# Attention values as one run of 256-column pairs, two buffers of turned units, and the queries turned in the projection's bank

## The chip, the cores and the metric

One core of a Trainium2 chip runs the whole kernel. Its engines are TensorE (PE: matmuls and transposes, with its weight loads on PEld), VectorE (DVE), ScalarE (ACT), GpSimd (POOL) and SyncE (SP, which issues most transfers). Each works through its own list of instructions in order and waits at semaphores for the others. The metric is the device time of one execution in microseconds.

## The reference

One block of a hybrid network over 512 latent tokens and 256 context tokens, width 1024: a state-space scan and an attention beside it share one input projection and one output projection; then a mixture of experts. The change touches only the attention over 768 keys (context and latent) with 16 query heads in 4 groups, and what of the output projection follows it:

```python
def one_block(q_blk):
    s = jnp.einsum('bqhgd,bkhd->bhgqk', q_blk, k, preferred_element_type=F32) * scale
    pr = jax.nn.softmax(s, axis=-1).astype(v.dtype)
    return jnp.einsum('bhgqk,bkhd->bqhgd', pr, v)
```

## The kernel before, in words

The stages follow one another: input projection and scan, attention, experts. `attention()` (L896) works on 16 units, each a pair of a key group `kv` and a tile `t` of 128 queries (the table `order`); a unit has four heads. The loop at its end runs over steps of one head, and `step(i, start, n)` says which unit is at a stage that begins `start` steps after the unit's first head:

- step 0: `scores(u, g)`. Four matmuls write 768 columns of scores into one of two slots of `pss_`; the slots share the middle one of three PSUM banks. DVE takes the row maximum (L956), ACT the exponential with the row sum (L957), into `P`. At the second head `q_stack` prepares the next unit's queries (POOL L923, ACT L925, DVE L926); at the fourth `q_turn(u + 1)` transposes them (L934) in a bank "b", and ACT copies them out twice (L936, L937).
- step 2: `turn(j)`. P of four heads is 24 blocks of 128 x 128; six groups of four are transposed (L963) into a bank "b" and copied to `PT` by DVE (L967) or ACT (L965) in turn. A group can straddle two heads.
- steps 4 and 6: `values(u, j)`. For two heads at a time, 12 matmuls of 128 columns: the heads `2j` and `2j+1` go to the upper and lower 64 columns of the array.
- steps 6 and 7: `norms` (reciprocal sums) and `finish` (scaling by a transposed copy of them, L992 to L999).
- steps 9 and 10: `project(u, n)`, six matmuls of 512 columns into bank "t" (for the last two units into `pss_`), which DVE adds to the running sum (L1017).

`pb(tag)` hands out PSUM banks: there are two banks "b", and one each of "t" and "s". A bank is handed to its users in the order in which the program asks for it, and each waits until the one before has been read. Bank "t" has other users: the eight tiles of `out_group(1, n)` (L814, twelve matmuls each, added by DVE at L830), which is the scan's share of the output projection; and near the end the transposes, logits and tables of the expert router. The tiles of `out_group(1, n)` are written in the program ahead of the call of `attention()` (L1249):

```python
    at = tc.cur_priority
    for n in range(2):
        with rank(at + LAG):
            out_group(1, n)
```

The order on each engine is not the order of the program text: a scheduler takes the instructions by priority (`rank` sets it) and by when it expects them to be ready, and so strews the tiles of `out_group(1, n)` among the first units' heads. Which user of a bank comes first is fixed by the text all the same. `mm` (L109) is the helper through which most matmuls go, so its rows are told apart by their tiles: `s<-kT,hxl` or `s<-hxl` are scores, `v<-hxh,hxl` and `s<-hxh,hxl` values, `t<-whi,a` and `t<-wlo,a` out_group(1), `t<-whi,ah`, `t<-ml,ah` and the like projections.

## Time and profile before

| | |
|---|---|
| three runs | 889.95, 896.88, 919.74 us; median 896.88 |
| profiled execution | 891.73 us, span 889.9 us |
| mean granted TensorE clock | 0.967 |
| busy | PE 798.8 us (90%), DVE 630.3 (71%), ACT 455.0 (51%), POOL 268.0 (30%) |
| chain that ended last | PE 59%, DMA 14%, DVE 11%, ACT 6% |
| attention | first exponential at 409.57 us of the span, last at 647.52 |

The busy shares are means over stages with different limits: in the input projection and in the experts transfers of weights run at over 300 GB/s, in attention at far less. So the windows of attention are read by themselves, and its time is counted from exponential to exponential (L957), 64 of them, four a unit; the exponential of unit u's head g is number 4u + g from 0.

### The profile page before, as it was taken

What the parts mean: (1) busy time and instruction counts of PE and PEld (TensorE: products, weight loads), DVE (VectorE), ACT (ScalarE), POOL (GpSimd) and SP (SyncE); (2) the same over time, 40 slices, a digit from 0 to 9 for tenths busy, and PEclk for the clock granted to TensorE, in tenths of its full rate; (3) what the DMA queues carried; (4) which work ended last, traced back from release to release, by engine and by line L of the source; (5) the groups of instructions that cost most, each with busy time, mean ns of one, the idle gap of its engine ahead of it and who ended that gap; (6) DMA issues with size and microseconds to landing.
All of it is one profiled execution on the core that took longest, in us unless ns stands there. A gap on an engine that the chain in (4) does not pass through costs nothing.

```text
span 889.9 us, 14409 instructions
## 1 busy us (share of the span) xinstructions
PE 798.8 (90%) x5328; PEld 604.5 (68%) x5328; DVE 630.3 (71%) x1042; ACT 455.0 (51%) x870; POOL 268.0 (30%) x202
## 2 busy tenths in 40 slices
PE   6998999898989989899999899999982999999783
PEld 3696676566777568677777777787862777777562
DVE  3576665786857896573646566666987999889677
ACT  2253442656743353364544645656461766777452
POOL 0012212313321052510159344600011355544421
PEclk8999999999999999999999999999995999999997
DMA  9966987446522144566052111300459999999964
GB/s 308 321 193 230 299 292 251 124 125 199 144 73 80 30 130 131 194 197 207 18 194 73 36 35 42 119 13 1 143 195 324 343 342 341 338 325 344 341 181 167
DMA packets 112369, 165.59 MB, mean 186 GB/s; under 512 B 13032, under 2 KB 78088, under 8 KB 112296
## 3 DMA queue, kind: packets, MB, share of 16 engines
q1 hardware_dynamic: 105720, 141.76, 49.2%
q0 software_dynamic: 6288, 21.84, 8.6%
q8 instruction: 42, 0.69, 0.3%
q10 hardware_dynamic: 288, 1.05, 0.3%
q14 instruction: 31, 0.25, 0.1%
HBM read 142.41 MB, written 22.21 MB: 185 GB/s over the span
## 4 chain that ended last, share of the span: by engine, by line
PE 59%; DMA 14%; DVE 11%; ACT 6%; issue 5%; POOL 3%; SPq 1%; DVEq 0%; POOLq 0%; ACTq 0%
PE a L109 24%; PE s L109 13%; PE t L109 7%; PE b L963 3%; DMA wraw<-in_w_mod_dram 3%; PE v L109 3%; PE b L109 3%; DMA bc<-csd 2%; PE m L109 2%; DVE acc L475 2%; ACT hxh L957 1%; PE b L1368 1%; DMA wraw<-in_w_up_dram 1%; DMA ml<-in_w_down_dram 1%; DMA ml<-in_w_up_dram 1%
## 5 line engine op out<-in xcount | busy, mean ns | idle before, releaser
L76 ACT ACTIVATE whi<-wraw 128x1024 fp32r<-128x1024 f32 (+1 forms) x100 | 104.2, 1045 | 62.7 <-PE a L109 31.9
L78 DVE TENSOR_TENSOR wlo<-wraw,whi 128x1024 fp32r<-128x1024 f32 (+1 forms) x75 | 95.7, 1282 | 29.3 <-ACT whi L76 29.3
L78 POOL TENSOR_TENSOR wlo<-wraw,whi 128x1024 fp32r<-128x1024 f32 (+1 forms) x20 | 49.3, 2464 | 150.6 <-ACT whi L76 132.2
L956 DVE TENSOR_REDUCE mx<-s 128x1 f32<-128x768 f32 x64 | 61.1, 955 | 29.6 <-PE s L109 24.4
L957 ACT ACTIVATE hxh<-s,mx 128x768 f32<-128x768 f32 x64 | 57.5, 898 | 41.1 <-DVE mx L956 39.5
L475 DVE SCALAR_TENSOR_TENSOR acc<-u,cols,acc 128x770 f32<-128x770 f32 (+1 forms) x48 | 55.4, 1153 | 30.3 <-ACT acc L467 24.3
L109 PE MATMUL a<-whi,hxh 128*128 128x512 f32 (+2 forms) x176 | 69.1, 394 | 1.5 <-ACT hxh L265 1.5
L109 PE MATMUL a<-wlo,hxh 128*128 128x512 f32 (+2 forms) x176 | 69.1, 393 | 0.2 <-DVE wlo L78 0.2
L109 PE MATMUL a<-whi,hxl 128*128 128x512 f32 (+2 forms) x176 | 67.9, 387 | 0.0
L109 PE MATMUL a<-hxh,whi 128*128 128x512 f32 (+1 forms) x176 | 62.5, 355 | 0.0
L109 PE MATMUL a<-hxl,whi 128*128 128x512 f32 (+1 forms) x176 | 62.2, 354 | 0.0
L109 PE MATMUL a<-hxh,wlo 128*128 128x512 f32 (+1 forms) x176 | 61.7, 350 | 0.0
L963 PE MATMUL b<-cst,hxh 128*128 128x128 f32 x384 | 58.7, 277 | 1.7 <-DVE hxh L967 0.5
L592 ACT ACTIVATE bc<-bc,lb 128x128 f32<-128x128 f32 x128 | 40.5, 390 | 23.6 <-POOL bc L589 20.4
L963 PEld LDWEIGHTS b<-cst,hxh 128*128 128x128 f32 x384 | 43.5, 141 | 11.4 <-ACT hxl L937 4.0
L967 DVE COPY hxh<-b 128x512 f32<-128x512 f32 x48 | 33.0, 687 | 16.9 <-PE b L963 16.7
L109 PE MATMUL a<-whi,xh 128*128 128x512 f32 x102 | 44.4, 436 | 0.0
L589 POOL TENSOR_SCALAR_AFFINE_SELECT bc<-bc 128x512 f32<-128x512 f32 x32 | 26.5, 835 | 52.4 <-DMA bc<-csd 50.4
L109 PE MATMUL a<-whi,xl 128*128 128x512 f32 x102 | 41.3, 405 | 0.0
L109 PE MATMUL a<-wlo,xh 128*128 128x512 f32 x102 | 41.2, 404 | 0.0
L1417 POOL DMA_INDIRECT acc<-y,rowi x15 | 28.2, 1881 | 40.8 <-DVE wlo L78 19.4
L109 PEld LDWEIGHTS a<-wlo,hxh 128*128 128x128 f32 x176 | 33.8, 192 | 9.9 <-issue 5.3
(467 smaller groups left out, 2123.2 us busy)
## 6 DMA issues: line engine op xcount, KB each, us to landing
wraw<-in_w_mod_dram SPq DMA_DIRECT2D x32, 512.0 KB
wraw<-in_w_in_dram SPq DMA_DIRECT2D x30, 512.0 KB
wraw<-in_w_down_dram SPq DMA_DIRECT2D x22, 512.0 KB
wraw<-in_w_gate_dram SPq DMA_DIRECT2D x40, 256.0 KB
wraw<-in_w_up_dram SPq DMA_DIRECT2D x40, 256.0 KB
mraw<-in_w_mod_dram SPq DMA_DIRECT2D x32, 256.0 KB
bc<-csd SPq DMA_DIRECT2D x32, 256.0 KB
wraw<-in_w_out_dram SPq DMA_DIRECT2D x15, 512.0 KB
```

Source lines behind the costliest of these rows:

```text
L76: self.nc.scalar.activation(hi, raw, AF.Copy)
L78: self.lo_engine(i).tensor_sub(lo, raw, hi.bitcast(F32))
L109: return PE.matmul(o, lhsT=a, rhs=b, start=first, stop=last)
L475: V.scalar_tensor_tensor(a, uk, wk_, a, op0=OP.mult, op1=OP.add)
L589: G.affine_select(bc[:, d], bc[:, d], pattern=[[0, 4], [sg, 128]], compare_op=OP.is_ge, fill=-1e30, base=0, channel_multiplier=-sg)
L592: S.activation(bc[:, d, h, :], bc[:, d, h, :], AF.Exp, bias=lb[:, c, h0 + h:h0 + h + 1])
L956: V.tensor_reduce(m, x, axis=AX, op=OP.max, negate=True)
L957: S.activation(P[:, g * 768:g * 768 + 768], x, AF.Exp, bias=m, accum_out=sm[u][:, g:g + 1])
L963: PE.transpose(p[:, i * 128:(i + 1) * 128], P[:, (4 * j + i) * 128:(4 * j + i + 1) * 128], ident)
L967: V.tensor_copy(PT[:, o], p)
L1368: PE.transpose(p[:, j * 128:(j + 1) * 128], x[:, k * 128:(k + 1) * 128], ident)
L1417: G.indirect_dma_start(out=acc, out_offset=bass.IndirectOffsetOnAxis(ap=rows, axis=0), in_=y, in_offset=None, compute_op=OP.add)
```

## The change

- `turn(u, g)` works on one head, one step after it: two groups of three transposes, the first copied by DVE, the second by ACT (384 columns each).
- `P` becomes a ring of two heads in a tile of its own; the room that it had holds a second buffer of turned units.
- `values(u)` runs once all four heads are turned, at step 5: 12 matmuls of 256 columns (two heads beside each other), key blocks in reverse, into one column half of the array and the other in turn.
- `norms` and `finish` move to steps 5 and 6; heads 0, 1 now lie in one half and 2, 3 in the other, so the sums and the weight rows of the output projection are arranged to match (`attn_piece`: two transfers of 64 partitions each for a weight piece instead of one).
- `q_turn(u)` for u > 0 takes bank "t" instead of one of the banks "b".

```diff
 
+    def attn_piece(kv, n):
+        def views(t):
+            for gp in range(2):
+                r = 1024 + kv * 256 + gp * 128
+                yield t[gp * 64:gp * 64 + 64], I["w_out"][r:r + 128, n * 512:n * 512 + 512].rearrange(
+                    "(j d) n -> d j n", j=2)
+        return views, 2, 512
+
     def scaled(i, w):
...
     wout = Stream(nc, wp, [piece(4 * g + k0, n) for g in range(2) for n in range(2) for k0 in (0, 2)]
-                  + [piece(8 + 2 * kv, n) for kv in range(4) for n in range(2)], 1, 2, held=1, scale=scaled,
+                  + [attn_piece(kv, n) for kv in range(4) for n in range(2)], 1, 2, held=1, scale=scaled,
                   lo_engine=lambda i: V if i < 8 else G, place=place,
...
         big = hxp.tile([128, 6144], F32, name="hxh")
-        P, PT = (big[:, o:o + 3072] for o in (0, 3072))
-        PTh = PT.rearrange("p (g k q) -> p g k q", g=4, k=6)
+        PT = [big[:, o:o + 3072] for o in (0, 3072)]
+        PS = 2
+        Ps = wo.tile([128, 768 * PS], F32, name="P", bufs=1)
         more = hxp.tile([128, 6144], F32R, name="hxl")
...
         def q_turn(u, qs):
-            p = pb("b", F32R)
+            p = pb("t", F32R) if u else pb("b", F32R)
             for g in range(4):
...
             V.tensor_reduce(m, x, axis=AX, op=OP.max, negate=True)
-            S.activation(P[:, g * 768:g * 768 + 768], x, AF.Exp, bias=m, accum_out=sm[u][:, g:g + 1])
-
-        def turn(j):
-
-            p, o = pb(), slice(j * 512, (j + 1) * 512)
-            for i in range(4):
-                PE.transpose(p[:, i * 128:(i + 1) * 128], P[:, (4 * j + i) * 128:(4 * j + i + 1) * 128], ident)
-            if j % 2:
-                S.activation(PT[:, o], p, AF.Copy)
-            else:
-                V.tensor_copy(PT[:, o], p)
+            at = (4 * u + g) % PS * 768
+            S.activation(Ps[:, at:at + 768], x, AF.Exp, bias=m, accum_out=sm[u][:, g:g + 1])
+
+        def turn(u, g):
+
+            at = (4 * u + g) % PS * 768
+            for h in range(2):
+                p, o = pb()[:, 0:384], slice(g * 768 + h * 384, g * 768 + h * 384 + 384)
+                for i in range(3):
+                    f = at + (3 * h + i) * 128
+                    PE.transpose(p[:, i * 128:(i + 1) * 128], Ps[:, f:f + 128], ident)
+                if h:
+                    S.activation(PT[u % 2][:, o], p, AF.Copy)
+                else:
+                    V.tensor_copy(PT[u % 2][:, o], p)
 
...
 
-        def values(u, j):
+        def values(u):
 
             kv = order[u][0]
-            if j == 0:
-                po[u] = pb("s") if u % 2 else pss.tile([128, 512], F32, name="v")
-            for k in range(6):
-                for a in range(2):
-                    mm(po[u][a * 64:a * 64 + 64, j * 128:j * 128 + 128], vv[:, k, kv * 64:(kv + 1) * 64],
-                       PTh[:, 2 * j + a, k], k == 0, k == 5)
+            po[u] = pb("s") if u % 2 else pss.tile([128, 512], F32, name="v")
+            w = PT[u % 2].rearrange("p (g k q) -> p g k q", g=4, k=6)
+
+            for k in reversed(range(6)):
+                for a in (1, 0):
+                    mm(po[u][a * 64:a * 64 + 64, 0:256], vv[:, k, kv * 64:(kv + 1) * 64], w[:, 2 * a:2 * a + 2, k], k == 5, k == 0)
 
...
             V.reciprocal(rc, sm.pop(u))
-            rcb = wo.tile([128, 4, 64], F32, name="rcb", bufs=1)
-            S.activation(rcb, rc[:, :, None].to_broadcast([128, 4, 64]), AF.Copy)
-            return rcb.rearrange("p g d -> p (g d)")
+            rcb = wo.tile([128, 2, 2, 64], F32, name="rcb", bufs=1)
+            S.activation(rcb, rc.rearrange("p (g j) -> p j g", j=2)[:, :, :, None].to_broadcast([128, 2, 2, 64]), AF.Copy)
+            return rcb
 
...
             for j in range(2):
-                PE.transpose(p[:, j * 128:(j + 1) * 128], rcb[:, j * 128:(j + 1) * 128], ident)
+                PE.transpose(p[:, j * 128:(j + 1) * 128], rcb[:, j].rearrange("p g d -> p (g d)"), ident)
             rb = wo.tile([128, 256], F32, name="rb")
...
                     q_turn(u + 1, qs.pop(u + 1))
-            u, g = step(i, 2, 4)
+            u, g = step(i, 1, 4)
             if u is not None:
-                for j in ((0,), (1, 2), (3,), (4, 5))[g]:
-                    turn(j)
-            u, g = step(i, 4, 3)
-            if u is not None and g != 1:
-                values(u, g // 2)
-            u, g = step(i, 6, 1)
+                turn(u, g)
+            u, g = step(i, 5, 1)
+            if u is not None:
+                values(u)
+            u, g = step(i, 5, 1)
             if u is not None:
                 outs[u] = norms(u)
-            u, g = step(i, 7, 1)
+            u, g = step(i, 6, 1)
             if u is not None:
```

PE's order around the eight tiles of out_group(1), before, from the exponential of unit 0's head 3 on (`t<-whi,a`, `t<-wlo,a` are its matmuls, `b<-identr,qs` is q_turn(2)):

```order
1737 L109 MATMUL s<-kT,hxl 128x512 x2
1738 L109 MATMUL s<-kT,hxl 128x256 x2
1739 L963 MATMUL b<-cst,hxh 128x128 x6
1740 L109 MATMUL t<-whi,a 128x512 x2
1741 L109 MATMUL t<-wlo,a 128x512
1742 L109 MATMUL t<-whi,a 128x512
1743 L109 MATMUL v<-hxh,hxl 64x128 x4
1744 L109 MATMUL s<-kT,hxl 128x256 x2
1745 L109 MATMUL s<-kT,hxl 128x512 x2
1746 L963 MATMUL b<-cst,hxh 128x128 x4
1747 L109 MATMUL v<-hxh,hxl 64x128 x7
1748 L934 MATMUL b<-identr,qs 128x128 x4
```

And of the change, from the transposes of head 3 to the second q_turn:

```order
1735 L109 MATMUL t<-whi,a 128x512 x2
1736 L109 MATMUL v<-hxh,hxl 64x256 x12
1737 L1005 MATMUL v<-cst,rcb 128x128 x2
1738 L109 MATMUL t<-wlo,a 128x512
1739 L109 MATMUL t<-whi,a 128x512 x2
...
1782 L109 MATMUL t<-wlo,a 128x512
1783 L109 MATMUL t<-whi,a 128x512
1784 L943 MATMUL t<-identr,qs 128x128 x4
1785 L109 MATMUL s<-kT,hxl 128x512 x2
1786 L109 MATMUL s<-kT,hxl 128x256 x2
1787 L943 MATMUL t<-identr,qs 128x128 x4
```

Before, a few matmuls of a tile (here four, at most ten) stood between two heads' scores, and the tiles were spread over the heads of units 0 to 3. Now rows 1738 to 1783 are matmuls of these tiles alone, 46 rows or 68 matmuls, and q_turn(1) (`t<-identr,qs`, row 1784) and the scores of unit 1 (rows 1785, 1786) come behind them.

PE's order around a q_turn of a steady unit, before (`b<-identr,qs`, with the projection's second half ahead of the scores):

```order
1995 L109 MATMUL t<-whi,ah 128x512
...
2000 L109 MATMUL t<-whi,al 128x512
2001 L109 MATMUL s<-hxl 128x256 x2
2002 L109 MATMUL s<-hxl 128x512 x2
2003 L934 MATMUL b<-identr,qs 128x128 x4
2004 L963 MATMUL b<-cst,hxh 128x128 x4
2005 L992 MATMUL v<-cst,rcb 128x128 x2
2006 L109 MATMUL s<-hxh,hxl 64x128
2007 L963 MATMUL b<-cst,hxh 128x128 x4
```

And of the change (`t<-identr,qs`):

```order
1997 L109 MATMUL t<-ml,ah 128x512
1998 L109 MATMUL t<-whi,al 128x512
1999 L109 MATMUL s<-kT,hxl 128x256 x2
2000 L109 MATMUL s<-kT,hxl 128x512 x2
2001 L976 MATMUL b<-cst,P 128x128 x2
2002 L943 MATMUL t<-identr,qs 128x128 x4
2003 L976 MATMUL b<-cst,P 128x128 x4
2004 L109 MATMUL t<-whi,ah 128x512
2005 L109 MATMUL t<-ml,ah 128x512
2006 L109 MATMUL t<-whi,al 128x512
2007 L109 MATMUL t<-whi,ah 128x512
2008 L109 MATMUL s<-kT,hxl 128x512 x2
```

The q_turn, the projection ahead of it and the projection behind it now share bank t; a projection's first half is split around the scores (rows 2004 to 2007 and, not shown, 2011 and 2012), and the values stand in two runs behind the next two heads' transposes.

PE's order near the end, at the last q_turn, before (`t<-Ab,trib` is a tile of the router in bank t):

```order
2222 L109 MATMUL s<-hxl 128x512 x2
2223 L934 MATMUL b<-identr,qs 128x128 x4
2224 L963 MATMUL b<-cst,hxh 128x128 x4
2225 L992 MATMUL s<-cst,rcb 128x128 x2
2226 L109 MATMUL v<-hxh,hxl 64x128
2227 L963 MATMUL b<-cst,hxh 128x128 x4
2228 L109 LDWEIGHTS trib
2229 L109 MATMUL t<-Ab,trib 128x16
2230 L963 MATMUL b<-cst,hxh 128x128 x4
2231 L109 MATMUL v<-hxh,hxl 64x128 x4
2232 L109 MATMUL s<-hxl 128x512 x2
```

And of the change:

```order
2177 L109 MATMUL s<-hxl 128x512 x2
2178 L976 MATMUL b<-cst,P 128x128 x12
2179 L109 MATMUL v<-hxh,hxl 64x256 x2
2180 L109 LDWEIGHTS trib
2181 L109 MATMUL t<-Ab,trib 128x16
2182 L109 MATMUL v<-hxh,hxl 64x256 x4
2183 L943 MATMUL t<-identr,qs 128x128 x4
2184 L109 MATMUL v<-hxh,hxl 64x256 x4
2185 L109 MATMUL s<-hxl 128x512
2186 L109 MATMUL v<-hxh,hxl 64x256
2187 L109 MATMUL s<-hxl 128x512
2188 L109 MATMUL s<-hxl 128x256 x2
```

The q_turn stood ahead of the router's matmul, in a bank of its own; now it stands behind it and waits for the same bank. The scores of the last unit (rows 2185, 2187 and 2188) follow the q_turn.

## Rows read from the trace of the kernel before

**Rows 1.** The page, part 1: busy us (share) xinstructions.

```profile
PE 798.8 (90%) x5328; PEld 604.5 (68%) x5328; DVE 630.3 (71%) x1042; ACT 455.0 (51%) x870; POOL 268.0 (30%) x202
```

**Rows 2.** Windows of attention: length, busy per engine, clock, DMA share, GB/s.

```profile
409.57:478.46 68.89, 67.46 (x449) 51.86 (x449) 36.97 (x54) 36.08 (x71) 25.70 (x13) 1.00 0.36 115
536.84:550.66 13.82, 13.48 (x110) 10.81 (x108) 8.79 (x14) 7.69 (x18) 5.35 (x4) 1.00 0.04 11
550.66:607.30 56.64, 54.74 (x436) 43.55 (x432) 36.60 (x54) 33.08 (x71) 17.33 (x11) 1.00 0.19 57
613.51:647.52 34.01, 33.66 (x295) 27.35 (x291) 28.41 (x69) 19.76 (x42) 1.75 (x3) 1.00 0.28 94
647.52:655.67 8.15, 8.15 (x104) 6.93 (x101) 6.51 (x15) 3.82 (x8) 1.14 (x2) 1.00 0.13 17
```

**Rows 3.** Timeline, fourth head of unit 8: start us, us, engine, line, instruction.

```profile
545.34 0.87 PE L109 MATMUL s<-kT,hxl 128*128 128x256 f32 x4
546.04 0.46 PE L934 MATMUL b<-identr,qs 128*128 128x128 f32 x4
546.31 0.96 DVE L956 TENSOR_REDUCE mx<-s 128x1 f32<-128x768 f32 x1
546.54 0.60 ACT L936 ACTIVATE hxl<-b 128x512 fp32r<-128x512 f32 x1 [1.99 <-PE b L934]
547.03 0.58 ACT L937 ACTIVATE hxl<-b 64x512 fp32r<-64x512 f32 x1
547.51 0.89 ACT L957 ACTIVATE hxh<-s,mx 128x768 f32<-128x768 f32 x1
548.54 0.98 PE L109 MATMUL s<-kT,hxl 128*128 128x512 f32 x4 [0.22 <-ACT hxh L957]
```

**Rows 4.** Groups by line and shape, 409 to 652 us: busy, mean ns, idle before.

```profile
L967 DVE COPY hxh<-b 128x512 f32<-128x512 f32 x48 | 33.0, 687 | 16.9 <-PE b L963 16.7
L109 PE MATMUL v<-hxh,hxl 128*64 128x128 f32 x384 | 31.3, 280 | 0.1
L965 ACT ACTIVATE hxh<-b 128x512 f32<-128x512 f32 x48 | 28.5, 594 | 23.2 <-PE b L963 23.0
```

**Rows 5.** Timeline, bank t changing hands between two tiles, at two places.

```profile
436.55 0.39 PE L109 MATMUL t<-wlo,a 128*128 128x512 f32 x1
436.78 0.39 PE L109 MATMUL t<-whi,a 128*128 128x512 f32 x1
437.21 0.69 DVE L830 TENSOR_TENSOR y<-y,t 128x512 f32<-128x512 f32 x1
437.95 0.50 PE L109 MATMUL t<-whi,a 128*128 128x512 f32 x1
...
454.60 0.39 PE L109 MATMUL t<-whi,a 128*128 128x512 f32 x1
455.70 0.68 DVE L830 TENSOR_TENSOR y<-y,t 128x512 f32<-128x512 f32 x1
456.44 0.51 PE L109 MATMUL t<-whi,a 128*128 128x512 f32 x1 [0.57 <-DVE y L830]
```

**Rows 6.** Timeline, PE: values of unit 7's second half, then a projection.

```profile
541.12 0.43 PE L109 MATMUL s<-hxh,hxl 128*64 128x128 f32 x2
542.39 1.53 PE L109 MATMUL s<-hxh,hxl 128*64 128x128 f32 x22
543.85 0.50 PE L109 MATMUL t<-whi,ah 128*128 128x512 f32 x1
```

**Rows 7.** Timeline, around the exponentials 59 and 60.

```profile
633.31 0.89 ACT L957 ACTIVATE hxh<-s,mx 128x768 f32<-128x768 f32 x1
633.71 0.19 DVE L1196 TENSOR_TENSOR tmp<-A,t 128x32 f32<-128x32 f32 x1 [0.20 <-PE t L109]
636.88 0.68 DVE L1146 TENSOR_TENSOR x<-x,a 128x512 f32<-128x512 f32 x1
637.00 0.91 ACT L957 ACTIVATE hxh<-s,mx 128x768 f32<-128x768 f32 x1 [1.54 <-DVE al L999]
```

## The prediction, made before the changed kernel was run

> **What bounds the kernel now.** I read the page's busy line first [rows 1]: TensorE (PE) is at work for 90% of the span, so a share says nothing yet about a change inside one stage. The change touches attention alone, from the first exponential at 409.57 us to the last at 647.52. So the windows over that stage come next [rows 2]: PE is busy for 67.46 of 68.89 us in units 0 to 3, for 13.48 of 13.82 in unit 8, 33.66 of 34.01 at the end, at a granted clock of 1.00 throughout. Every gap between heads is filled by PE work of another unit.
>
> Then one head in order of time [rows 3]. Scores start at 545.34, DVE's max at 546.31, ACT's exp at 547.51, the next scores at 548.54 (they wait for that exp, since the two score slots share a bank). This ring of scores, max, exp needs 3.2 us a head, four heads a unit: 12.8 us. Unit 8 takes 13.82, so two limits lie close together: PE's sum of work and the ring. What decides is what stands between two scores in PE's order.
>
> **The change, part by part.**
>
> *Values.* Now 24 matmuls of 128 columns in two halves; the two column halves of the array run side by side. The first matmul of a half stands alone, 0.43 us for two records, the other eleven (22 records) take from 542.39 to 543.85, 1.46 us [rows 6]: about 3.7 us a unit. Twelve of 256 columns move as many columns: 11 pairs of records in 1.46 us is about 0.11 a pair with the entry taken off, 0.22 for twice the columns, 12 pairs 2.6 us, and about 0.25 us of entry for each of the two runs that PE's order makes of them: 3.1. PE is spared 0.6 us a unit (0.8 from the 3.9 us of busy time that 31.3 us over eight units are [rows 4]).
>
> *Turns.* The 24 transposes a unit stay; 3 copies of 512 on DVE (687 ns) and 3 on ACT (594 ns) [rows 4] become 4 and 4 of 384. Three quarters of the first is 515 and 445 ns as a lower bound, the full price an upper one; near the lower, DVE has the same 2.1 us a unit and ACT the same 1.8. Nothing, as neither is the ring's next step: a copy runs while PE makes scores. Two buffers of turned units take away the wait of a turn for the values before it; no row shows such a wait that costs over 0.3 us. Norms and finish come one step sooner with the same instructions: nothing. The weight pieces of the projection come as two transfers of half the partitions, eight more issues on SP: the DMA engines are busy for 0.04 to 0.36 of these windows [rows 2] and a piece is asked for units ahead, which hides it; if it came late, it would stop the projection once in four units.
>
> *The queries' turn in bank t.* This is the part that I put the sum on. Bank t is a single one, handed out in program order. The eight tiles of out_group(1) are asked for before attention() is called, so q_turn(1) gets the bank after the last of them. In PE's order as built (shown above) it stands behind six of these tiles that come in one block after head 3 of unit 0, and the scores of unit 1 wait for it. Before, these tiles were strewn between the heads of units 0 to 3.
>
> From the first exp: three heads at 3.2, 9.6 us. Then, from head 3's exp on: exp 0.9, six transposes 0.7, four matmuls of the first tile with their wait 1.2, values 3.1, finish 0.3, eight matmuls 1.9. Then the bank changes hands: the last matmul of a tile starts at 436.78, DVE's addition at 437.21, the next tile's first at 437.95 [rows 5]: 1.17 us instead of the 0.23 from 436.55 to 436.78, 0.94 us that nothing fills. So 0.9, then five tiles of 12 x 0.23 = 2.8 with 0.94 behind each, 18.7. Then the q_turn's own chain [rows 3]: turn at 546.04, copies at 546.54 and 547.03, the second done at 547.61: 1.57; second half of the scores 0.7, max 1.0, exp 0.3: 3.6. Sum from exp 3 to exp 4: 31.3. Unit 1 then has nothing left to fill it and goes at the ring's 12.8; units 2 and 3 at the 13.5 of the steady state below. Together 9.6 + 31.3 + 12.8 + 27.0 = 80.7 us against 68.9 [rows 2]: **+11.8**. Bounds: +5, if most of the hand-overs and the chain are made good by PE work that values no longer need; +16, if DVE comes late to each, as where the last matmul starts at 454.60, the addition at 455.70 and the next tile at 456.44, 1.84 us [rows 5], 0.67 more for six.
>
> *Steady units 4 to 13.* A head's interval is PE's list between scores, if above the ring's 3.2. After head 3: scores 0.9, two transposes, q_turn, four transposes, then the projection, which waits until ACT has emptied bank t, 1.57 us after the q_turn's start, and four of its matmuls: 3.6. Next: scores 0.9, transposes 0.7, two matmuls 0.5, six values 1.5: 3.6. Then two heads at the ring's 3.15. That is 13.5 against 13.8: -0.3 for ten units, **-3**. Bounds: -8, if all 0.8 us that PE is spared come off each unit, and +7, if the bank is late by 0.67 in each. In the trace DVE's addition starts 0.43 us after the last matmul in most places, so I stay near the order's own sum.
>
> *The end.* In unit 14 q_turn(15) stands behind the router's tile in bank t, whose reader on DVE (the L1196 of before) has a chain of small operations ahead of it, two copies and three additions of 0.68 [rows 7]. In order after head 59's max: 3.3 us until the router's operand is there, 1.3 more until the reader is done, then the 3.6 of the q_turn's chain: 8.3 from exp to exp, where it now takes 3.69 (633.31 to 637.00) [rows 7]. With q_turn(14) behind the transposes for the logits, about 1.4 more: **+6** on the 34.01 us of that window [rows 2], none to +9. After the last exp PE reached finish(15) in 8.15 us [rows 2]; with turns of a single head left, exp 0.9, transposes 0.7, a copy 0.6, values 3.1 and three matmuls make 6.1: **-2**. Behind it the MoE stage streams weights and moves as a whole.
>
> Sum: 11.8 - 3 + 6 - 2 = **+12.8 us** on the profiled execution's 891.73: 904.5. That execution lies 5.2 us under the median of the three runs shown, 896.88 (at the median it would be 909.7). I say **907**, between the two. Under about 2% of change a measurement of this kernel can't be told from none; +12.8 is 1.4%.
>
> **The rivals.**
>
> 1. *PE is the bound and collects.* For it: 97 to 99% busy in every window [rows 2]. Then the ten units give 0.8 each, -8, and the block loses only +6; with +5 and -2 for the end the sum is +1: 893 to 898. Against it: the ring's 12.8 a unit leaves no room for more than 1.0, and the list after head 3 still holds the wait for ACT.
>
> 2. *Slower: bank t is handed on late.* Its place is DVE between the projection's addition and whatever was issued ahead of it. If each of six hand-overs in the block and eleven q_turns pays 0.67 us more [rows 5], that is +11.4 on top: +24, 921. It decides where DVE's addition starts later than about 0.6 us after the last matmul. Against it: in the block DVE has little else to do. The Trainium skill (Perfetto Trace Analysis, Optimizing Tensor Performance, Matmuls) has a rule that speaks against the change in just this place: independent matmul groups should rotate through different PSUM banks, so that one's evacuation lies beside the next one's matmuls. The trace agrees in the block, where 0.94 us a tile stay unfilled; by the rule every turn of the queries would pay, which is this rival's 921, and by the rows of the steady units, where the addition comes at once, it is the forecast's 907.
>
> 3. *Faster: the block costs nothing.* The same PE work has to be done anyway; if the six tiles merely move forward and units 1 to 3 win back all of it, and each unit gives 0.8 for 16 units with 2 at the tail, -15 and 878. Against it: a ring that stands still for 27 us can't be caught up in three units of at most 1.0 to 4 us slack each.
>
> 4. *256 columns don't run side by side.* Then the change doesn't do what it says: values 24 x 0.22 = 5.3 a unit, 2.2 more than I took, in 14 units +31: 936. Against it: the 128-column pairs do [rows 6].
>
> **How the numbers follow.** Forecast 0.50, rival 1 0.22, rival 2 0.17, rival 3 0.07, rival 4 0.04. Range 890 to 923: from rival 1's lower side to the whole of rival 2, leaving out 3 and 4 and some of the edges. Slower by over 2% (915 and more): rivals 2 and 4 and a fifth of the forecast's spread, 0.30. Faster by over 2% (under 879): rival 3, 0.06. Within: 0.64.
>
> **What the changed profile would show.** The interval of about 31 us between the fourth and fifth exp, with PE on t tiles and a gap of 0.9 at each first matmul; unit 1 at 12.8 and a steady unit at 13.5; values of 256 columns in 24 records of 2.6 us without entries; an interval of 8 us before exp 60. I am wrong if units 0 to 3 take under 74 us, or the steady unit under 13.0.

## The result and the profile after

Four runs of the changed kernel took 913.73 to 918.48 us, median 917.65; four of the kernel before 889.95 to 919.74, median 896.42. The ratio is **1.025** (95% interval 1.0205 to 1.0296): slower, by more than a measurement of this kernel is uncertain. (The 919.74 us of before was an execution in the chip's slower state, 3% above the fastest, and the ratio leaves it out.) The profiled execution took 918.48 us, 26.75 over the one of before, at a mean granted clock of 0.963 (0.967 before).

The busy line of the page (busy us, share, instructions) answers to [rows 1]:

```profile
PE 800.1 (87%) x4944; PEld 587.9 (64%) x4944; DVE 639.4 (70%) x1058; ACT 458.7 (50%) x886; POOL 270.0 (29%) x202
```

PE has 384 records fewer (24 a unit, as the values are half as many instructions), yet as much busy time as before. So the 26.75 us are time in which PE waits or runs at a lower clock, and the question is where.

The lines of the changed kernel are numbered anew: the max is L965, the exp L967, the q_turn L943 with its copies L945 and L946, out_group's addition L838. L935 and L1012 are DVE's subtractions that make the lower parts of the next queries and of the attention's output. A weight piece is scaled on POOL (L785, before L777), its upper part is made on ACT (L76) and its lower part on POOL (L78).

The windows of attention answer (length, busy us of each engine, granted clock, DMA share, GB/s): units 0 to 3, the stretch from exp 16 to exp 54, the end to the last exp, and from there to the last finish. They answer to [rows 2].

```profile
411.16:494.83 83.67, 68.56 (x377) 50.26 (x375) 41.14 (x60) 37.66 (x76) 34.62 (x16) 0.96 0.35 100
494.83:639.27 144.44, 127.78 (x791) 91.21 (x791) 89.96 (x144) 77.22 (x173) 43.93 (x25) 0.95 0.13 39
639.27:678.20 38.93, 34.08 (x260) 24.33 (x258) 29.45 (x76) 22.16 (x47) 2.32 (x4) 1.00 0.23 82
678.20:684.05 5.85, 4.94 (x42) 3.24 (x38) 5.60 (x10) 1.89 (x5) 0.58 (x1) 1.00 0.15 63
```

The stretch from exp 16 to exp 54 has no single row among those of before; here it is, with units 5 and 6 of it behind:

```profile
478.46:613.51 135.05, 129.15 (x1020) 102.95 (x1017) 85.62 (x136) 75.46 (x163) 53.03 (x29) 1.00 0.14 42
492.69:523.03 30.34, 27.37 (x219) 21.79 (x216) 16.72 (x29) 17.21 (x38) 12.85 (x7) 1.00 0.08 27
```

| stretch (profiled executions) | before | after | difference | predicted |
|---|---|---|---|---|
| to the first exp | 409.57 | 411.16 | +1.6 | 0 |
| units 0 to 3 (exp 0 to 16) | 68.89 | 83.67 | +14.8 | +11.8 |
| exp 16 to 54 | 135.05 | 144.44 | **+9.4** | **-3** |
| exp 54 to 63 | 34.01 | 38.93 | +4.9 | +6 |
| after exp 63 | 244.2 | 240.3 | -3.9 | -2 |
| all | 891.73 | 918.48 | +26.75 | +12.8 |

**The block.** The interval from exp 3 to exp 4, then the first one of unit 1:

```profile
420.64:454.59 33.95, 25.32 (x120) 17.25 (x118) 10.71 (x15) 10.99 (x18) 11.05 (x5) 0.97 0.36 102
454.59:459.10 4.51, 3.48 (x12) 3.08 (x13) 2.72 (x3) 2.25 (x7) 4.43 (x3) 0.50 0.70 194
```

33.95 us between two exps, as the order had shown; and when the ring starts again the granted clock is 0.50, the lower of TensorE's two levels (1.2 instead of 2.4 GHz), and the step takes 4.51 instead of 3.2: its four score matmuls take 1.65 us (0.97 in unit 8), and its max waits some 0.75 us for L935, which takes 1.81 beside POOL. The end of the block in order of time (start, us, engine, line, instruction):

```profile
444.71 0.69 DVE L838 TENSOR_TENSOR y<-y,t 128x512 f32<-128x512 f32 x1 [3.17 <-PE t L109]
...
448.29 4.67 POOL L78 TENSOR_TENSOR ml<-wraw,whi 128x1024 fp32r<-128x1024 f32 x2 [2.76 <-ACT whi L76]
448.55 0.69 DVE L838 TENSOR_TENSOR y<-y,t 128x512 f32<-128x512 f32 x1 [3.16 <-PE t L109]
449.30 0.53 PE L943 MATMUL t<-identr,qs 128*128 128x128 f32 x4 [0.78 <-DVE y L838]
...
451.28 1.97 DVE L935 TENSOR_TENSOR qs<-q,qs 128x256 fp32r<-128x256 f32 x1 [2.03 <-ACT qs L934]
...
453.00 1.06 ACT L76 ACTIVATE wraw<-wraw 128x1024 fp32r<-128x1024 f32 x1 [1.75 <-POOL ml L78]
453.17 0.95 DVE L965 TENSOR_REDUCE mx<-s 128x1 f32<-128x768 f32 x1
454.09 0.60 ACT L945 ACTIVATE hxl<-t 128x512 fp32r<-128x512 f32 x1
454.59 0.89 ACT L967 ACTIVATE P<-s,mx 128x768 f32<-128x768 f32 x1
```

The additions of these two tiles lie 3.84 us apart (3.74 in the sum); so do those of the others, but for one pair 4.68 apart, where DVE's L78 (432.03, 1.23 us) stood ahead of the addition (433.18). The q_turn starts when the last has freed the bank. Its chain to the exp takes 5.29 us (449.30 to 454.59) where I took 3.6. The scores are done at 451.7, but the max starts only at 453.17, some 1.3 us late, since DVE's L935 stands ahead of it: it takes 1.97 us and ends 0.29 us after POOL's L78 (451.28 + 1.97 against 448.29 + 4.67). Then a weight piece (L76) and the next q_turn's copy stand ahead of the exp on ACT, which is some 0.4 us more.

**Units 5 and 6.** They took 38.16 us against 30.34; PE's clock fell here too:

```profile
509.73:547.89 38.16, 29.55 (x168) 21.01 (x166) 18.14 (x29) 16.63 (x38) 13.08 (x7) 0.87 0.08 19
516.46:524.38 7.92, 1.98 (x15) 1.57 (x14) 2.72 (x5) 2.43 (x5) 2.34 (x1) 1.00 0.27 66
524.38:529.22 4.84, 3.35 (x12) 2.67 (x12) 2.12 (x6) 2.85 (x8) 0.00 (x0) 0.51 0.06 19
529.22:535.79 6.57, 6.44 (x32) 3.93 (x34) 1.15 (x3) 1.38 (x5) 0.61 (x1) 0.58 0.02 6
```

The timeline of the interval of 7.92:

```profile
512.81 2.40 POOL L78 TENSOR_TENSOR wraw<-wraw 128x1024 fp32r<-128x1024 f32 x1
515.24 1.76 SPq L53 DMA_DIRECT2D wraw<-in_w_out_dram  x2
520.57 2.34 POOL L785 TENSOR_TENSOR wraw<-wraw,wx 128x1024 f32<-128x1024 f32 x1 [5.36 <-DMA wraw<-in_w_out_dram]
522.94 1.06 ACT L76 ACTIVATE whi<-wraw 128x1024 fp32r<-128x1024 f32 x1 [5.49 <-POOL wraw L785]
523.90 0.58 ACT L945 ACTIVATE hxl<-t 128x512 fp32r<-128x512 f32 x1
524.38 0.89 ACT L967 ACTIVATE P<-s,mx 128x768 f32<-128x768 f32 x1
525.41 0.79 PE L109 MATMUL s<-hxl 128*128 128x512 f32 x1 [5.96 <-ACT P L967]
```

It is read from the bottom up. PE waits 5.96 us for an exp; the exp stands on ACT behind L76, which makes the upper part of a weight piece; that waits 5.49 for POOL, POOL for the transfer, and the transfer for the buffer that POOL's subtraction of the piece before (L78) freed at 515.2. So a chain of weights, which nobody needs for another unit, stops the ring because it lies ahead of an exp in ACT's list. Behind it PE works at 0.51 and 0.58 of its clock, and the next intervals are 4.84 and 6.57.

The kernel before has this chain too, one exp later in ACT's list:

```profile
509.30 1.06 ACT L76 ACTIVATE whi<-wraw 128x1024 fp32r<-128x1024 f32 x1 [2.84 <-POOL wraw L777]
510.26 0.88 ACT L957 ACTIVATE hxh<-s,mx 128x768 f32<-128x768 f32 x1
```

There ACT waits 2.84 us for POOL, and the interval that ends with this exp takes 6.94 us, the longest of unit 5; the clock stays at 1.00.

**Units 7 to 9.** Three intervals of 3.1 to 3.5 us and a fourth of 4.05 to 4.49 where 3.15 was summed. The end of unit 7:

```profile
556.02 2.36 POOL L1033 TENSOR_TENSOR x<-x,wx 128x1024 f32<-128x1024 f32 x1 [2.06 <-DVE x L1030]
557.07 1.59 DVE L1012 TENSOR_TENSOR al<-o,ah 128x256 fp32r<-128x256 f32 x1
558.46 2.45 POOL L1035 TENSOR_TENSOR x<-x,wlo 128x1024 f32<-128x1024 f32 x1
559.37 1.82 DVE L935 TENSOR_TENSOR qs<-q,qs 128x256 fp32r<-128x256 f32 x1 [0.15 <-ACT qs L934]
561.11 0.95 DVE L965 TENSOR_REDUCE mx<-s 128x1 f32<-128x768 f32 x1
562.15 0.90 ACT L967 ACTIVATE P<-s,mx 128x768 f32<-128x768 f32 x1 [0.81 <-DVE mx L965]
```

Two DVE subtractions that take 0.42 us elsewhere take 1.59 and 1.82 and both end 0.28 us after a POOL operation (557.07 + 1.59 against 556.02 + 2.36; 559.37 + 1.82 against 558.46 + 2.45). The max and the exp wait behind the second.

**The end.** From exp 59 to exp 60, answering to [rows 7]:

```profile
659.30 0.90 ACT L967 ACTIVATE P<-s,mx 128x768 f32<-128x768 f32 x1
661.58 0.17 DVE L1197 TENSOR_TENSOR Ab<-A 128x16 bf16<-128x16 f32 x1
662.38 0.18 PE L109 MATMUL t<-Ab,trib 128*128 128x16 bf16 x1
662.60 0.19 DVE L1208 TENSOR_TENSOR tmp<-A,t 128x32 f32<-128x32 f32 x1
663.51 0.53 PE L943 MATMUL t<-identr,qs 128*128 128x128 f32 x4
...
666.77 0.96 DVE L965 TENSOR_REDUCE mx<-s 128x1 f32<-128x768 f32 x1 [3.30 <-PE s L109]
667.82 0.90 ACT L967 ACTIVATE P<-s,mx 128x768 f32<-128x768 f32 x1 [2.67 <-DVE mx L965]
```

8.52 us instead of 3.69: router's operand, router's matmul, its reader, then the q_turn, in that order.

### The profile page after: what moved, and what is told of

The parts are those of the page before. It is cut to its first block, busy times and chain, and to the rows that moved or that the text cites. A ratio compares the mean times of both kernels' runs of the same rounds, so it can differ in the third digit from the quotient of the medians.

```text
span 916.7 us, 13634 instructions
## 1 busy us (share of the span) xinstructions
PE 800.1 (87%) x4944; PEld 587.9 (64%) x4944; DVE 639.4 (70%) x1058; ACT 458.7 (50%) x886; POOL 270.0 (29%) x202
## 4 chain that ended last, share of the span: by engine, by line
PE 59%; DVE 16%; DMA 9%; ACT 7%; issue 5%; POOL 2%; SPq 1%; DVEq 0%; POOLq 0%; ACTq 0%
PE a L109 26%; PE s L109 12%; PE t L109 6%; DMA wraw<-in_w_mod_dram 3%; PE b L976 3%; PE b L109 3%; PE m L109 2%; DVE acc L475 2%; ACT P L967 2%; DMA bc<-csd 2%; DVE wlo L78 2%; PE v L109 2%; PE b L1380 1%; ACT hxh L978 1%; DVE mx L965 1%
## 5 line engine op out<-in xcount | busy, mean ns | idle before, releaser
L76 ACT ACTIVATE whi<-wraw 128x1024 fp32r<-128x1024 f32 (+1 forms) x100 | 104.1, 1045 | 67.4 <-PE a L109 33.2
L78 DVE TENSOR_TENSOR wlo<-wraw,whi 128x1024 fp32r<-128x1024 f32 (+1 forms) x75 | 96.2, 1288 | 30.1 <-ACT whi L76 29.4
L965 DVE TENSOR_REDUCE mx<-s 128x1 f32<-128x768 f32 x64 | 61.2, 956 | 48.2 <-PE s L109 46.1
L78 POOL TENSOR_TENSOR wlo<-wraw,whi 128x1024 fp32r<-128x1024 f32 (+1 forms) x20 | 49.3, 2464 | 151.1 <-ACT whi L76 131.3
L978 ACT ACTIVATE hxh<-b 128x384 f32<-128x384 f32 x64 | 31.2, 488 | 82.4 <-PE b L976 82.3
L967 ACT ACTIVATE P<-s,mx 128x768 f32<-128x768 f32 x64 | 57.5, 899 | 6.4 <-DVE mx L965 6.3
L976 PE MATMUL b<-cst,P 128*128 128x128 f32 x384 | 56.2, 278 | 3.1 <-ACT P L967 2.7
L976 PEld LDWEIGHTS b<-cst,P 128*128 128x128 f32 x384 | 45.8, 143 | 8.8 <-ACT P L967 3.5
L1429 POOL DMA_INDIRECT acc<-y,rowi x15 | 28.4, 1893 | 41.9 <-DVE wlo L78 19.7
```

Of the source, the lines that this page charges most:

```text
L76: self.nc.scalar.activation(hi, raw, AF.Copy)
L78: self.lo_engine(i).tensor_sub(lo, raw, hi.bitcast(F32))
L965: V.tensor_reduce(m, x, axis=AX, op=OP.max, negate=True)
L967: S.activation(Ps[:, at:at + 768], x, AF.Exp, bias=m, accum_out=sm[u][:, g:g + 1])
L976: PE.transpose(p[:, i * 128:(i + 1) * 128], Ps[:, f:f + 128], ident)
L978: S.activation(PT[u % 2][:, o], p, AF.Copy)
```

## The experiments

Each edit is to the changed kernel, unless it says otherwise. Ratios are to the kernel before, timed beside it on the same chip, with 95% intervals. "0 to 63" is from the first exp to the last, in the profiled execution (238.0 us before, 267.0 after).

### The queries' bank

**e1_turn_in_b** undoes the bank alone.

```diff
-            p = pb("t", F32R) if u else pb("b", F32R)
+            p = pb("b", F32R)
```

> The change with one thing undone: the queries of every unit are turned in a bank b again. Theory A (bank t is the whole loss): the interval of 33.95 us between the fourth and fifth exponential goes back to under 4, the first four units take 66 to 69 us instead of 83.7, the stalls of units 13 to 14 go, and the rest of the change shows its own worth: 885 to 893, a little under the kernel before. Rival B (the turns by single heads or the halved weight pieces cost as well): 898 to 905, still above the kernel before, with the long intervals of units 5 and 6 (7.9, 4.8, 6.6 us) kept.

Measured: 1.0048 (1.0022 to 1.0074), median 896.4 us, between the two expectations; 0 to 63 in 246.3 us. Most of the loss is the bank's.

**e2_before_with_t** puts the bank alone into the kernel before.

```diff
-            p = pb("b", F32R)
+            p = pb("t", F32R) if u else pb("b", F32R)
```

> The kernel before with one part of the change alone: the queries of units 1 to 15 are turned in bank t. Theory A: the same block of out_group(1) stands before the scores of unit 1, so about the whole loss, +20 to +28 us: 917 to 925. Rival C (bank t hurts only together with the turns by head, which leave PE less to do in the waits): +5 to +12, 902 to 908.

Measured: 1.0201 (1.0160 to 1.0243), median 908.0 us, again between the two. The two parts add up, within these intervals: 2.0% for the bank and 0.5% for the rest against 2.5% for both. Of the 20.7 us that 0 to 63 grows (258.7), units 0 to 3 hold 19.7 and the end 1.3; exp 16 to 54 takes 134.8, against 135.1 before. Units 0 to 3:

```profile
408.37:496.94 88.57, 76.44 (x476) 56.10 (x474) 41.32 (x57) 38.08 (x72) 35.40 (x17) 0.96 0.27 92
```

**e3_t_from_unit_4** and **e5_t_4_to_13** say in which units.

```diff
# e3
+            p = pb("t", F32R) if u > 3 else pb("b", F32R)
# e5
+            p = pb("t", F32R) if 4 <= u < 14 else pb("b", F32R)
```

> The change with the queries of units 1 to 3 turned in bank b and those of units 4 to 15 in bank t as in the change. It takes out the block alone. Theory A1 (the block is most of the loss, the later units pay little): first four units 66 to 69 us, total 899 to 904. Theory A2 (the later turns in t cost as much, by the wait on the projection, on the router and by the stall of units 5 and 6): 905 to 910.

> The change with the queries turned in bank t for units 4 to 13 alone, and in bank b for units 0 to 3, 14 and 15. Against the run with t from unit 4 (905.6) it takes out the turns that stand behind the router's tiles. If these are the cost that remains at the end, unit 14 goes from 21.4 us to about 14 and unit 13 from 16.9 to 15: 896 to 899. If the end is slow for DVE's list of router operations, wherever the queries are turned, it stays at 903 to 906.

Measured: e3 1.0169 (1.0127 to 1.0211), median 905.6 us; e5 1.0119 (1.0077 to 1.0160), median 904.2, where the end goes as first expected and the total does not. In their traces units 0 to 3 take 71.1 and 71.4 us instead of 83.7 (that is the block), the end 41.9 in e3 and 33.9, as before, in e5 (that is the router's tile); but exp 16 to 54 takes 143.8 and 143.9 in both, against 138.6 in e1. So beside the rest of the change bank t costs 5.2 us in the units where I had forecast a gain, and units 5 and 6 hold it: 37.3 us in e3, 37.4 in e5, 31.6 in e1. About half of it is only moved, since units 0 to 3 take 73.9 us in e1, 2.4 more than in e5: 0 to 63 differs by 2.8 us between these two. And in the kernel before bank t costs nothing in these units (e2). By the ratios, of the 2.0% some 0.8 is units 1 to 3 (1.025 to 1.0169), 0.5 units 14 and 15, 0.7 the units between, each step uncertain by about half a per cent.

### The stall in units 5 and 6

**e4_whole_pieces** asks whether the halved weight pieces make the late transfer.

```diff
-                  + [attn_piece(kv, n) for kv in range(4) for n in range(2)], 1, 2, held=1, scale=scaled,
+                  + [piece(8 + 2 * kv, n) for kv in range(4) for n in range(2)], 1, 2, held=1, scale=scaled,
```

> The change with the attention rows of the output weights loaded in one transfer of 128 partitions a piece as before, not in two of 64 (the rows then stand in the old order, so the attention's share of the output is computed with permuted weights). If the halved transfers are behind the stall of units 5 and 6 (issue at 515.24, scaling on POOL not before 520.57), it shortens by 1.5 to 2 us, and with the clock that falls behind it by up to 6: 911 to 916. If they cost nothing: 917 to 918.

Measured: 1.0302 (1.0251 to 1.0354), the interval of unit 5 still 7.8. The halved pieces are not the cause of it. Unit 6 takes 16.1 us instead of 18.7, which stays unexplained. (Its total isn't a gauge: the weight rows are permuted, so the experts get other data.)

**e9_after_lo_on_dve** shortens the chain: the lower part of every weight piece is made on DVE, so that the buffer comes free sooner. POOL still scales the piece.

```diff
-                  lo_engine=lambda i: V if i < 8 else G, place=place,
+                  lo_engine=lambda i: V, place=place,
```

> The change with one thing moved: the low parts of the attention's output weights (pieces 8 to 15) are subtracted on DVE, 1.2 to 1.3 us each, instead of on POOL, 2.4. In the change the stall of units 5 and 6 (38.2 us for both where two steady ones take 27) ends a chain of POOL's subtraction, the transfer into the slot that it frees, POOL's scaling, and ACT's copy, which stands ahead of an exponential. If that chain is the cause, both together fall to 28 to 31 us and the clock stays up: 907 to 912. If the transfer alone sets it, 36 to 38 us and 916 to 918.

Measured: 1.0172 (1.0099 to 1.0244), median 908.0 us, 0.8% under the changed kernel, though the intervals overlap. Units 5 and 6:

```profile
506.87:539.49 32.62, 28.56 (x168) 20.46 (x166) 21.00 (x31) 16.70 (x38) 9.36 (x5) 0.90 0.10 23
```

32.62 instead of 38.16, somewhat over the 28 to 31 expected, and the clock falls here all the same (0.90). But the interval of 7.92 is 3.62: L76 stands ahead of the same exp and waits 0.51 us for POOL. So the stall is the chain's. It doesn't need bank t: with the queries in b, e6 below has an interval of 7.93 at the same place (L76 waits 5.03 us there), and the kernel before its 6.94. In e1 L76 stands behind that exp, and the stall is gone.

### The rest, 0.5%

**e6_b_values_128**: e1 with values of 128 columns, as before.

```diff
+            for j in range(2):
+                for k in reversed(range(6)):
+                    for a in (1, 0):
+                        mm(po[u][a * 64:a * 64 + 64, j * 128:j * 128 + 128], vv[:, k, kv * 64:(kv + 1) * 64], w[:, 2 * a + j, k], k == 5, k == 0)
```

> The change with the queries turned in bank b (896.4) and the values in one go but as 24 matmuls of 128 columns instead of 12 of 256. If the width itself gives nothing (the same columns, two records each, side by side either way): 895 to 899. If each wide matmul saves an entry, as the prediction's 0.6 us a unit has it, 16 units lose up to 10: 902 to 906.

Measured: 1.0054 (1.0031 to 1.0077), median 895.8 us, the same as e1; units 11 and 12 take 13.24 and 13.25 us, against 13.5. In the total the width gives nothing. The attention is laid out otherwise, though: units 0 to 3 take 68.5 us instead of 73.9, and exp 16 to 54, with the 7.93 of unit 5, 142.6 instead of 138.6.

**e7_b_quiet_pool**: e1 without three POOL operations a tile.

```diff
-                G.tensor_tensor(us_[t], us_[t], held["g_a"], op=OP.mult)
-                G.tensor_scalar(x, x, ALPHA, None, op0=OP.mult)
-                G.tensor_add(us_[t], us_[t], x)
```

> The change with the queries turned in bank b (896.4), and with the three operations on POOL left out that scale the output rows and add x to them during units 6 to 9 (the result lacks that). In the trace DVE's subtractions take 1.6 to 2.4 us instead of 0.42 there and hold up the maximum at the end of these units. If POOL's work beside them is the reason, they fall to 0.42, the last interval of units 6 to 9 goes from 4.5 to 3.2 us, and the total to 889 to 892. If not, the intervals stay and the total is 895 to 897.

Measured: 0 to 63 in 238.6 us, 7.7 under e1, as fast as before; its total (1.0373) says nothing of attention, since the experts get other data, and 277.3 us pass behind the last exp instead of 247.3. The same subtractions with POOL quiet:

```profile
545.99 0.43 DVE L1012 TENSOR_TENSOR al<-o,ah 128x256 fp32r<-128x256 f32 x1 [0.18 <-ACT ah L1011]
548.17 0.42 DVE L935 TENSOR_TENSOR qs<-q,qs 128x256 fp32r<-128x256 f32 x1 [0.65 <-ACT qs L934]
```

The fourth interval of units 6 to 8 falls from 4.5 to 3.2 to 3.3, which with the rest of these units makes 4.9 us; 4.8 more come off units 3 and 4, where one of the three, L1034, runs three times in a row on POOL in e1 (8.41 us); unit 9 gives back 1.8. The mean of L935 over attention is 574 ns here, 882 in e1, 1141 in the changed kernel, 575 (as L926) before, where most of these subtractions fell between POOL's operations.

**e8_b_lag_300**: e1 with the tiles of out_group(1) set later.

```diff
-    LAG, HOLD, WX = 150, 40, 3
+    LAG, HOLD, WX = 300, 40, 3
```

> The change with the queries turned in bank b (896.4) and the eight tiles of out_group(1) set later in the order (LAG 300 instead of 150), so that fewer of them stand in one lump in unit 2. With the lump of 57 matmuls spread over two units more, the PE idle time of units 3 to 4 fills: 888 to 893, and perhaps under the kernel before (892.1). If the projections behind them in bank t come late and hold up the ring: 898 to 905.

Measured: 1.0075 (1.0037 to 1.0112), median 897.8 us. Units 0 to 3 take 66.0 us instead of 73.9, exp 16 to 54 143.9 instead of 138.6: units 3 and 4 have the tiles now, at 26.6 and 22.3 us. Nothing won.

### Other ways around POOL

e10 puts DVE's two subtractions on POOL, e11 the lower parts of the weights on DVE, e12 both; e13 puts the three operations of e7 on DVE, e14 these and the lower parts. All have the queries in b.

```diff
# e10, e12
+            G.tensor_sub(qs[:, :, 1], heads(q, 4), f32(qs[:, :, 0]))
...
+            G.tensor_sub(l, o, f32(h))
# e11, e12, e14
+                  lo_engine=lambda i: V, place=place,
# e13, e14
+                V.tensor_tensor(us_[t], us_[t], held["g_a"], op=OP.mult)
+                V.tensor_scalar(x, x, ALPHA, None, op0=OP.mult)
+                V.tensor_add(us_[t], us_[t], x)
```

> The change with the queries turned in bank b (896.4), and with the two subtractions of 256 columns (queries, attention output) on POOL instead of DVE. With DVE free of operations that POOL's slow down, the last interval of units 6 to 9 goes from 4.5 to about 3.3 us: 890 to 893. If POOL's queue of 2.4 us operations makes the queries late instead: 895 to 902.

> The change with the queries turned in bank b (896.4), and the low parts of the weights on DVE throughout. POOL is busy for 19.58 of unit 3's 19.66 us there; freed of it, units 3 to 6 (67 us) go to 58 to 61: 888 to 891, a little under the kernel before (891.5). If DVE's 1.3 us operations stand ahead of maxima and cost the same again: 894 to 898.

> The last two together, queries turned in bank b: low parts of the weights on DVE, the two subtractions of 256 columns on POOL. If both costs are real and apart: 883 to 888, under the kernel before by 0.4 to 1%. If they are one cost moved from one engine to the other: 890 to 896.

> The change with the queries turned in bank b (896.4), and the three operations that scale the output rows and add x to them on DVE instead of POOL (1.2 us each there, 2.4 on POOL), with nothing left out. Theory: the last interval of units 6 to 9 falls from 4.5 to 3.2 to 3.6 us, since POOL is quiet beside DVE's subtractions, and DVE's own 3.7 us a unit fit into its idle time: first to last exponential 240 to 243 us instead of 246.3, total 889 to 893, level with the kernel before (890 to 892). Rival: DVE's operations stand ahead of the maxima and cost as much, 245 to 249 us and 896 to 899.

> The same with the low parts of the weights on DVE too. If POOL's work was all that kept the change without bank t above the kernel before: first to last exponential 238 to 241 us, total 886 to 890, at or under the kernel before. If the lump of out_group(1) in units 2 to 3 is a cost of its own (about 5 us more than before in units 0 to 3): 241 to 245 and 891 to 895.

| | ratio (95%) | 0 to 63, us |
|---|---|---|
| e10 | 1.0427 (1.0353 to 1.0500) | 275.9 |
| e11 | 1.0077 (1.0040 to 1.0114) | 244.6 |
| e12 | 1.0415 (1.0342 to 1.0488) | 272.2 |
| e13 | 1.0154 (1.0093 to 1.0214) | 252.7 |
| e14 | 1.0102 (1.0045 to 1.0159) | 248.6 |

None wins, and all but e11, whose rival expectation came true (median 895.6 us), are slower than either expectation had them. On POOL the subtractions queue behind its operations of 2.4 us and the ring waits for them (in e10 the last intervals of units 6 to 9 are 7.9 to 8.5 us, and unit 3 takes 32.6 instead of 19.7). On DVE the three operations stand before a max: in e13 the third intervals of units 6 to 9 take 5.3 to 7.9. One place in e13, where the work that took POOL 2.45 us takes DVE 1.22, and L935 is slow again, now beside a lower part of the weights on POOL (555.90 + 2.34 = 558.24; L935 ends at 558.52, again 0.28 later):

```profile
554.49 1.22 DVE L1035 TENSOR_TENSOR y<-y,wlo 128x1024 f32<-128x1024 f32 x1
...
555.90 2.34 POOL L78 TENSOR_TENSOR whi<-wraw,whi 128x1024 fp32r<-128x1024 f32 x1 [10.78 <-PE t L109]
...
556.95 1.57 DVE L935 TENSOR_TENSOR qs<-q,qs 128x256 fp32r<-128x256 f32 x1
```

No variant beat the kernel before.

## Why the prediction was wrong

**The sign, the block and the end were right.** The block was forecast at 31.3 us from exp 3 to exp 4 and took 33.95; units 0 to 3 lost 14.8 instead of 11.8. The 3.0 more are above all 1.7 in the q_turn's chain (5.29 for 3.6; 1.3 of it DVE's slow L935 ahead of the max), 1.4 in the five tiles ahead of the q_turn (20.06 us for 18.7, 0.8 of it in the one late addition), and 1.2 in unit 1 (13.95 for 12.8), where the clock was low and L935 slow again; the work ahead of these tiles gave back 0.4 and units 2 and 3 0.7. Taking bank t out of units 1 to 3 takes 12.6 us out of that window (e3). The wait before exp 60, forecast at 8.3, took 8.52; the end lost 4.9 of 6, and e5 gives all of it back in its window. The tail to the last finish was forecast at 6.1 and took 5.85.

**The step that failed is "Steady units 4 to 13: -3".** It came out at +9.4, outside its own bounds of -8 and +7 (the upper one is ten late hand-overs of the bank, which isn't what happened), and these 12.4 us are most of the 14 by which the sum fell short. The sum was right where nothing interferes: units 11 and 12 took 13.48 us, forecast 13.5, before 13.8. It failed because I worked out one undisturbed unit from unit 8 of before and multiplied it by ten. Without bank t the same stretch still loses 3.55 us (138.60 against 135.05, e1).

- Units 5 and 6 were to give 0.6 and lost 7.8: 8.4 of the miss. I had costed the weight pieces at nothing, since "a piece is asked for units ahead". The wait for a piece isn't the projection's, it is ACT's, and the exp is queued behind it. The trace of before showed this already, in the 6.94 us of unit 5; unit 8, from which I summed, has no such piece. e9 shows that the chain is the cause. What sets its price is where ACT's list has L76: ahead of exp 23 in the changed kernel, e3, e5 and e6 (it waits 5.03 to 5.50 us), behind that exp, but ahead of the next, in the kernel before (2.84), and behind that exp in e1, where it waits 1.34 us and costs the ring nothing. So bank t brings the ring under the chain here, but e6 comes under it without bank t; why the scheduler's list comes out one way or the other I didn't isolate.
- The other units were to give 2.4 and lost 1.6. "Then two heads at the ring's 3.15" left out that DVE's list between two maxima holds subtractions whose price depends on POOL; e7 takes that away in units 6 to 8, in a kernel with the queries in b. The Trainium skill (SBUF — State Buffer, Who interferes with whom) says why: DVE and GpSimd share one pair of SBUF ports under an exclusive lock, and a DVE instruction with two SBUF inputs contends with a GpSimd instruction that reads SBUF. The trace agrees: 1.59 and 1.82 us for 0.42, ending 0.28 us behind POOL's. In the changed kernel units 7 and 8 lose 0.45 us each by the side of before; units 4, 9 and 10, which lose 1.2 together, I didn't take apart.

**The rivals.** "Bank t is handed on late" had nearly the total (921), by luck, and the wrong place: four of the five tiles in the block lie about 3.85 apart, 0.1 over the sum and not 0.67, only one paid more (0.9), and where units 5 to 8 lose, PE waits for an exp and not for the bank. "PE is the bound and collects": from exp 16 to 54 PE is busy for 88% of the window, before for 96%. "The block costs nothing": unit 0 loses 29.2 us to it, and units 1 to 3, freed of the tiles, win back 14.4 (40.2 us instead of 54.6). That is half, and more than the 1.0 to 4 us a unit that I allowed there: unit 2 alone gives 11.1. "256 columns don't run side by side": 24 records take 2.81 us, near the 2.6 forecast and far from this rival's 5.3. (The rivals' totals don't stand on one base: 921 is counted from the median of 896.88, 936 from the profiled execution of 891.73.)

```profile
423.42 2.81 PE L109 MATMUL v<-hxh,hxl 128*64 128x256 f32 x24
```

I had looked for what frees PE, and the changed kernel does spare it work; but what decides here is the lists of ACT and DVE, in which the ring's max and exp stand behind others' work.

**What stays open.** Of e1's 0.5%, e7's window shows that leaving out POOL's three operations gives back 7.7 us of attention, but no version kept their result and won that time. e8 moves the tiles without a gain; the gather told of below adds about 3 us to e1's profiled execution and not to before's. Why ACT's list has the weight piece ahead of an exp in some versions and behind it in others is open too.

## What to carry to other kernels

Before a single-buffered bank is given to an operation that a ring waits for, list all users of it in the order of the program: the ring then waits for every user ahead, also for work that could have been done at any time. A steady stage is not one unit times ten: look at every unit of the trace of before for a long step (here 6.94 us in unit 5), and in each for what stands ahead of the ring's steps on *every* engine of the ring, and ask how late that could be if the ring moved. And an operation's price on DVE is that of its neighbourhood: look at what POOL does at the new place.

## What the runs showed of the hardware

**The clock falls in the middle of attention.** It was 1.00 throughout in the windows of before. In the changed kernel, behind the stall in which PE was idle for 5.96 us, it was granted at 0.51 and 0.58 for 11.4 us, and at 0.50 behind the block. Four score matmuls there and in unit 8:

```profile
532.96 1.65 PE L109 MATMUL s<-hxl 128*128 128x256 f32 x4
...
563.19 0.97 PE L109 MATMUL s<-kT,hxl 128*128 128x256 f32 x4 [0.28 <-ACT P L967]
```

So the work behind a stall can be slower too. How much that is here isn't shown: the first two intervals behind the stall (4.84 and 6.57) are 4.38 and 4.71 in e9, 2.3 us less, but there the clock fell as well, to 0.51 and 0.73, behind an interval in which PE was busy for 1.78 of 3.62 us. In e1, without the stall, it was 0.58 and 0.68 at the same place.

**A gather's issue on POOL took 4.42 us instead of 1.08.** It is the first one of the experts, in e1:

```profile
684.88 2.35 DVE L78 TENSOR_TENSOR wlo<-wraw,whi 128x1024 fp32r<-128x1024 f32 x2
684.90 4.42 POOL L1257 DMA_INDIRECT x<-t_d,toki  x1 [10.79 <-DVE wlo L78]
687.15 1.22 DVE L78 TENSOR_TENSOR wlo<-wx,whi 128x1024 fp32r<-128x1024 f32 x1
```

and in the kernel before:

```profile
678.70 1.08 POOL L1245 DMA_INDIRECT x<-t_d,toki  x1 [10.55 <-DMA t_d<-wlo]
678.94 2.39 DVE L78 TENSOR_TENSOR wlo<-wraw,whi 128x1024 fp32r<-128x1024 f32 x2
```

Where DVE's subtractions of SBUF tiles come first, by 0.02 us, the gather ends at 689.32, 0.95 us after the last of three of them in a row (687.15 + 1.22), and 0.95 is about what an undisturbed one takes; where the gather comes first, it is not held. It took 3.52 to 4.35 us in e5, e7, e8 and e10 to e14 too, and 1.09 to 1.74 in the changed kernel, e2, e3, e4, e6 and e9. So the order in which two operations start, here 0.02 us apart, seems to decide over some 3 us. No experiment here took this apart by itself.
